# The beginning of a decoder block: first weights loaded behind the first squares, norm1_g turned between two bursts of warming matmuls, and another order of the third row tile's statistics

## Chip, cores and metric

One Trainium2 chip, one core. The metric is the device time of one execution in microseconds (us); the kernel before took 797.62 us (median of three runs, 797.24 to 797.83).

## What is computed

A decoder block on x of 512 rows and 1024 columns, in float32. The places this case is about are the first RMSNorm and the first product:

```
def rmsnorm(x, g):
    y = xf * lax.rsqrt(jnp.mean(xf * xf, axis=-1, keepdims=True) + EPS)
    return (y * g).astype(x.dtype)

h = rmsnorm(x, norm1_g[l])
z = h @ w_in[l] + b_in[l]          # 1024 x 6656
z_glu, z_rx, z_rg, z_ga, z_gb = jnp.split(z, split_idx, axis=-1)
...                                # convolution branch, RG-LRU branch, gates, mix
x = x + m @ w_mix_out[l]
h = rmsnorm(x, norm2_g[l])
x = x + (jax.nn.silu(h @ ffn_w1[l]) * (h @ ffn_w3[l])) @ ffn_w2[l]
return rmsnorm(x, norm_f_g)
```

## The kernel before

Every product is made of three matmuls in the fp32r form: each operand is split into a high part h (a cast) and a low part l (the residue), and h·h, h·l and l·h are added up. Weights come in chunks of 128 x 1024 numbers (512 KB): loaded into a `raw` buffer (four of them), cast into the high half of an `hl` buffer, and the low half is formed by a subtraction. Chunk keys `in0`, `in8`, `in1` and so on are blocks of 128 columns of w_in; `in0` is the first chunk and `in8` the second.

x lies as four row tiles of 128 rows, each in two halves of 512 columns (`x00`, `x01` are the halves of tile 0, `x10`, `x11` of tile 1; without numbers they all read `x`). A row tile's statistics are two squares with a sum on ScalarE (L550, L556; they write a scratch tile, `n1j`, that nobody reads), a small scaling on VectorE (L551), a root on ScalarE (L557) and a reciprocal on VectorE (L558); then VectorE scales both halves in place (L595). `rstd_begin` is the first square with L551, `rstd_end` the rest. `turn_half` then turns two row tiles at once on TensorE (L574, tiles `tx`), ScalarE writes the high part times norm1_g (L582, `h10h` to `h17h`) and VectorE the residue (L583, `h10l` to `h17l`). norm1_g itself comes as 8 rows of 128 and is turned into columns of the tile `par` by a transpose and a copy (`rows_turned`, L517 and L518).

The beginning is written under a manual schedule: on TensorE, ScalarE, VectorE and SyncE instructions stand in the order in which the code issues them; GpSimd's order, and everything behind this block, is set by a scheduler. Before it, 21 matmuls of ones by ones (L506, each two passes) keep TensorE busy. In the block, row tiles 0 and 1 are turned, then the first two chunks are multiplied with them (`early_mm(0, 0)` gives `z0`, `early_mm(1, 0)` gives `z8`, both L534, with the eight matmuls by the low part of the weights last), then row tiles 2 and 3 are turned and the two products are done for them. The low part of `in0` is formed on GpSimd (L119); that of `in8` on VectorE, kept back by the class `Later` and issued at L652.

All loads are issued from SyncE's queue: four for tiles 0 and 1, the rows of norm1_g, chunks `in0` and `in8` (L167), four for tiles 2 and 3, the rows of the other parameters (L483), further chunks. An instruction that waits holds up all those behind it on its engine.

Of the kernel before, what the change touches and what calls it, by code (L numbers as in the profile page):

```python
# [8 lines left out]
F32 = mybir.dt.float32  # L9
# [4 lines left out]
P = 128  # L14
T = 512
# [18 lines left out]
RAW = 4  # L34
HL = 5
AHEAD = 4
WARM = 21

FEW, MANY = 32, 112

# [13 lines left out]
ROWS = [  # L54
    ("norm1_g", 8), ("lru_lambda", 10), ("b_in", 52), ("lru_ba", 10), ("lru_bx", 10),
    ("conv_dw_b", 8), ("conv_ln_g", 8), ("conv_ln_b", 8), ("conv_b_out", 8), ("lru_conv_b", 10),
    ("norm2_g", 8), ("lru_conv_w", 40), ("conv_dw_w", 248),
]
# [28 lines left out]
def tile_block(ctx, tc, a, out):  # L87
    nc = tc.nc
    pool = lambda name, bufs, **k: ctx.enter_context(tc.tile_pool(name=name, bufs=bufs, **k))
    consts = pool("consts", 1)  # L90
    raws = pool("raws", RAW)
# [24 lines left out]
    newest = {}  # L116
# [25 lines left out]
    def wchunk(key, src, kt, cols, where="hl", lo=pool_e, after=None):  # L142
        chunks.append((key, src, kt, cols, where, lo, after))

    class Later:

        def tensor_tensor(self, **operands):
# [2 lines left out]
    def emit_chunk(copy=act.copy, lo_by=None):  # L150
        if emitted[0] == GATES_AT:
            load_gates()
        key, src, kt, cols, where, lo, after = chunks[emitted[0]]
        emitted[0] += 1
        lo = lo_by or lo
        n = kt * cols
        if where == "made":
            raw = src()
        else:
            raw = raws.tile([P, 1024], F32, tag="raw", name=f"raw_{key}")  # L160
        rv = raw[:, :n]
        if where == "made":
            pass
        elif callable(src):
            src(raw)
        else:
            newest["load"] = nc.sync.dma_start(rv.rearrange("p (k n) -> p k n", k=kt), src).ins  # L167
        if where != "long":
            hl = hls.tile([P, 2, 1024], F32R, tag="hl", name=f"hl_{key}")
            h, l, _ = split_to(hl[:, 0, :n], hl[:, 1, :n], rv, lo, copy)  # L170
            if after:
                after(rv, h)
            held[key] = (h.rearrange("p (k n) -> p k n", k=kt), l.rearrange("p (k n) -> p k n", k=kt))
        else:
            held[key] = [
                split_to(longt(f"{key}h{i}", F32R), longt(f"{key}l{i}", F32R), rv[:, i * T : (i + 1) * T], lo)
                for i in range(2)
            ]
# [323 lines left out]


    wp = bank2("warm")
    for _ in range(WARM):
        pe.matmul(wp[:, :P], ones, ones, start=True, stop=True)  # L506

    first = [i for i, (lo, _, _) in enumerate(parts) if lo < n_first]
    load_x(0)
# [3 lines left out]
    def rows_turned(c0, c1):  # L513
        pt = bank2(f"par_ps{c0}")
        for c in range(c0, c1, P):
            m = min(P, c1 - c)
            pe.transpose(pt[:, c - c0 : c - c0 + m], rowt[row_at(c)[0]][:m, :P], ident[:m, :m])  # L517
        vec.tensor_copy(par[:, c0:c1], pt[:, : c1 - c0])  # L518
        return pt
# [25 lines left out]
    def rstd_begin(half, junk):  # L545

        i = n_stats[0]
        n_stats[0] += 1
        ss, r = stats[:, i, :2], stats[:, i, 2:3]
        act.activation(junk, half, AF.Square, accum_out=ss[:, 0:1])  # L550
        vec.tensor_scalar(out=ss[:, 0:1], in0=ss[:, 0:1], scalar1=1.0 / D, scalar2=EPS, op0=ALU.mult, op1=ALU.add)  # L551
        return ss, r

    def rstd_end(begun, half, junk):
        ss, r = begun
        act.activation(junk, half, AF.Square, accum_out=ss[:, 1:2])  # L556
        act.activation(r, ss[:, 1:2], AF.Sqrt, scale=1.0 / D, bias=ss[:, 0:1])  # L557
        vec.reciprocal(r, r)  # L558
        return r

    def rstd_of(halves, junk, between=None):
        begun = rstd_begin(halves[0], junk[0])
        if between:
            between()
        return rstd_end(begun, halves[1], junk[1])
# [22 lines left out]

    h1p = [pairt(f"h1{c}") for c in range(ND)]

    def norm1_rows(t, between=None):
        junk = [shortt(f"n1j{t}{h}") for h in range(2)]
        r = rstd_of(xt[t], junk, between)
        for h in range(2):
            vec.tensor_scalar(out=xt[t][h], in0=xt[t][h], scalar1=r, scalar2=None, op0=ALU.mult)  # L595

    HALVES = [slice(0, 256), slice(256, 512)]
    EARLY = 1
# [39 lines left out]

    ET = mybir.EngineType
    with tc.manual_schedule(engines={ET.PE, ET.Activation, ET.DVE, ET.SP}):  # L640
        norm1_rows(0)
        norm1_rows(1)
        rows_turned(0, ROWS[0][1])
        emit_to(1, vec.tensor_copy)
        turn_half("tx", xt, "norm1_g", h1p, 0, [bank, bank, bank, bank2])
        later = Later()
        emit_to(2, vec.tensor_copy, later)
        load_x(2)
        load_x(3)
        for i in first[1:]:  # L650
            load_rows(i)
        norm1_rows(2, lambda: vec.tensor_tensor(**later.operands))  # L652
        norm1_rows(3)
        for i in range(len(parts)):
            if i not in first:
                load_rows(i)
        early_mm(0, 0)
        early_mm(1, 0)
        turn_half("tx", xt, "norm1_g", h1p, 1, [bank2, bank, bank])
        emit_to(3)  # L660
        early_mm(0, 1)
        lru_factors(rows_turned(ROWS[0][1], n_first)[:, 2 * P :])
        emit_to(4)
        early_mm(1, 1)
        rows_turned(n_first, n_rows)
# [625 lines left out]
```

## Time and profile before

| what | value |
|---|---|
| median of three runs | 797.62 us (797.24 to 797.83) |
| the profiled execution: its time | 797.7 us |
| the profiled execution: span from first to last instruction | 795.9 us |
| TensorE, busy share of the span | 99% |
| VectorE, ScalarE, GpSimd | 85%, 59%, 29% |
| first turning (tiles 0 and 1) begins | 8.97 us |
| second turning (tiles 2 and 3) begins | 17.28 us |

Times in rows are microseconds from the start of the span. A timeline row gives start, duration, engine, line, operation, written and read tiles, shape, count, and in brackets the idle time of the engine before it with what ended it. In grouped rows the figures behind the bar are busy time in us and the mean of one record in ns; the ones after that are idle time before the group. A record of a matmul lasts longer than the distance to the next one, since matmuls overlap. SPq is SyncE's queue of DMA issues, PEld the weight loads of TensorE.

### The profile page before, as it was taken

Reading aid. Unit: us, or ns where it says so; the run is one execution under the profiler, and the core shown is the slowest. Engines: PE = TensorE matmul, PEld = TensorE weight load, DVE = VectorE, ACT = ScalarE, POOL = GpSimd, SP = SyncE. Lnnn points to the kernel's source line nnn. Section 1 sums busy time; section 2 is a strip of 40 time slices with the busy share of each in tenths; the row PEclk is TensorE's granted clock in tenths of the full one; section 3 lists DMA queues with packets and bytes.
Section 4 is the critical chain, followed back from the end, with each engine's and each line's share of the span. In section 5 each row is a group of like instructions: output and inputs, shape, how many; then the busy total and the mean of one; then the engine's idle time right before and its main releaser. Section 6 shows DMA issues by size and latency. Waiting matters only on the chain.

```text
span 795.9 us, 12177 instructions
## 1 busy us (share of the span) xinstructions
PE 789.2 (99%) x4369; PEld 690.5 (87%) x4369; DVE 673.2 (85%) x1020; ACT 471.7 (59%) x683; POOL 228.8 (29%) x181
## 2 busy tenths in 40 slices
PE   9999999999999999999999999999999999999997
PEld 8888888888888888888888898999999999888885
DVE  6699899999989988786787889978878887889757
ACT  6646585987768855563335575545455555577443
POOL 1855766797666856030000000000000000000000
PEclk9999999999999999999999999999999999999999
DMA  6945646487555664368847545566555553676652
GB/s 213 257 130 143 187 144 208 121 247 208 173 168 173 213 182 120 128 203 263 276 160 243 172 134 158 131 171 181 155 133 133 133 133 106 210 258 207 198 173 106
DMA packets 184604, 140.29 MB, mean 176 GB/s; under 512 B 14259, under 2 KB 162143, under 8 KB 184543
## 3 DMA queue, kind: packets, MB, share of 16 engines
q1 hardware_dynamic: 183103, 134.27, 55.2%
q0 software_dynamic: 1440, 5.24, 3.5%
q8 instruction: 34, 0.56, 0.3%
q14 instruction: 27, 0.22, 0.1%
HBM read 113.79 MB, written 18.64 MB: 166 GB/s over the span
## 4 chain that ended last, share of the span: by engine, by line
PE 99%; DVE 0%; issue 0%; ACT 0%
PE z L534 36%; PE or L953 13%; PE ft L1080 7%; PE yb L534 7%; PE fa L1080 7%; PE fr L1080 6%; PE ya L534 5%; PE mxr L953 5%; PE fe L1080 4%; PE g L827 3%; PE fb L1080 2%; PE f L534 2%; PE warm L506 1%; PE f L1106 1%; PE tx L574 1%; PE th L574 0%
## 5 line engine op out<-in xcount | busy, mean ns | idle before, releaser
L702 DVE SCALAR_TENSOR_TENSOR cv<-u,par,cv 128x511 f32<-128x511 f32 (+19 forms) x240 | 162.4, 730 | 5.0 <-ACT cv L699 4.7
L119 POOL TENSOR_TENSOR hl_in<-raw_in,hl_in 128x1024 fp32r<-128x1024 f32 x51 | 123.5, 2426 | 83.1 <-ACT hl_in L123 69.6
L355 POOL DMA_DIRECT2D raw_fb<-raw_fb x10 | 8.7, 874 | 298.4 <-DVE raw_fb L357 186.1
L119 POOL TENSOR_TENSOR ows<-ows 128x256 f32<-128x256 f32 x66 | 56.7, 861 | 37.7 <-DMA ows<-in_ffn_w_dram 34.7
L123 ACT CAST hl_ft<-raw_fb 128x1024 fp32r<-128x1024 f32 x40 | 41.8, 1048 | 32.5 <-DVE raw_fb L357 17.0
L123 ACT CAST hl_in<-raw_in 128x1024 fp32r<-128x1024 f32 x50 | 52.1, 1043 | 10.4 <-PE z L534 6.6
L119 DVE TENSOR_TENSOR hl_ft<-raw_fb,hl_ft 128x1024 fp32r<-128x1024 f32 x40 | 48.5, 1220 | 7.0 <-ACT hl_ft L123 6.9
L119 DVE TENSOR_TENSOR hl_fb<-raw_fb,hl_fb 128x1024 fp32r<-128x1024 f32 x30 | 36.6, 1221 | 9.5 <-ACT hl_fb L123 9.3
L357 DVE TENSOR_TENSOR raw_fb<-raw_fb,raw_fb 128x1024 f32<-128x1024 f32 x20 | 24.5, 1225 | 20.3 <-DMA raw_fb<-in_ffn_w_dram 20.0
L534 PE MATMUL z<-h10h,hl_in 128*128 128x512 f32 (+1 forms) x108 | 41.5, 385 | 0.0
L534 PE MATMUL z<-h17h,hl_in 128*128 128x512 f32 (+1 forms) x108 | 41.1, 381 | 0.0
L534 PE MATMUL z<-h13h,hl_in 128*128 128x512 f32 (+1 forms) x108 | 41.1, 381 | 0.0
L534 PE MATMUL z<-h15h,hl_in 128*128 128x512 f32 (+1 forms) x108 | 41.1, 381 | 0.0
L534 PE MATMUL z<-h14h,hl_in 128*128 128x512 f32 (+1 forms) x108 | 41.1, 381 | 0.0
L534 PE MATMUL z<-h16h,hl_in 128*128 128x512 f32 (+1 forms) x108 | 41.1, 381 | 0.0
L534 PE MATMUL z<-h12h,hl_in 128*128 128x512 f32 (+1 forms) x108 | 41.1, 381 | 0.0
L534 PE MATMUL z<-h11h,hl_in 128*128 128x512 f32 (+1 forms) x108 | 41.1, 381 | 0.0
L123 ACT CAST hl_fb<-raw_fb 128x1024 fp32r<-128x1024 f32 x30 | 31.4, 1047 | 8.9 <-PE mxr L953 3.7
L119 DVE TENSOR_TENSOR hl_ob<-raw_ob,hl_ob 128x1024 fp32r<-128x1024 f32 (+1 forms) x23 | 27.0, 1174 | 11.0 <-ACT hl_ob L123 10.9
L123 ACT CAST hl_ob<-raw_ob 128x1024 fp32r<-128x1024 f32 (+1 forms) x23 | 23.3, 1015 | 21.6 <-PE or L953 10.8
L1080 PE MATMUL fe<-hs_0h,hl_ft 128*128 128x256 f32 x160 | 30.7, 283 | 0.0
L1080 PE MATMUL ft<-hs_1h,hl_ft 128*128 128x256 f32 x160 | 30.4, 283 | 0.0
(1016 smaller groups left out, 2610.0 us busy)
## 6 DMA issues: line engine op xcount, KB each, us to landing
raw_in<-in_w_in_dram SPq DMA_DIRECT2D x52, 512.0 KB
raw_fb<-in_ffn_w_dram SPq DMA_DIRECT2D x96, 256.0 KB
ows<-in_ffn_w_dram SPq DMA_DIRECT2D x44, 256.0 KB
os<-ows SPq DMA_DIRECT2D x22, 512.0 KB
raw_ob<-in_ffn_w_dram SPq DMA_DIRECT2D x33, 256.0 KB
raw_ot<-os SPq DMA_DIRECT2D x33, 256.0 KB
raw_lo<-in_lru_w_out_dram SPq DMA_DIRECT2D x16, 320.0 KB
raw_fb<-raw_fb POOLq DMA_DIRECT2D x10, 512.0 KB, 4.6
```

The costliest lines, as they stand in the source:

```text
L119: return eng.tensor_tensor(out=o, in0=x, in1=y, op=ALU.subtract)
L123: copy(h, full)
L355: pool_e.dma_start(out=q, in_=y, accum_op=ALU.add)
L357: vec.tensor_tensor(out=q, in0=q, in1=y, op=ALU.add)
L506: pe.matmul(wp[:, :P], ones, ones, start=True, stop=True)
L534: pe.matmul(ps, l, r, start=i == 0, stop=i == n - 1)
L574: pe.transpose(ps[:, t * P : (t + 1) * P], src, ident)
L702: vec.scalar_tensor_tensor(out=acc[c][:, s:], in0=u[c][:, : T - s], scalar=dw(c, s), in1=acc[c][:, s:], op0=ALU.mult, op1=ALU.add)
L827: pe.matmul(ps, l, r, start=k == 0, stop=k == len(mms) - 1)
L953: pe.matmul(banks[i], l_[:, ts], r_, start=start and n == 0, stop=stop and n == 2, skip_group_check=again)
L1080: pe.matmul(ps[:, HALVES[i]], lw[:, 4 * i + c, :], rx_, start=not (again or i or c or m), stop=bool(i and c == 3 and m == 2), skip_group_c ...
L1106: pe.matmul(plain_1[:, cs], l, r, start=k == 0 and m == 0, stop=k == ND - 1 and m == 2)
```

## The change

Three things change in the beginning.

1. The scratch tile of row tile 0's two squares is no longer a short tile but the first 512 columns of the raw buffers of chunks `in0` and `in8` (`weight_room`). The loads of these chunks are issued later in the code (`load_ahead`), `in0` in two pieces, and each must wait until the square that writes its buffer is done: first half and second half of `in0` behind the first square, `in8` behind the second.
2. The 21 warming matmuls become 12 and 6, and the turning of norm1_g with its copy stands between them, ahead of row tile 1's statistics in the code.
3. `Later`'s subtraction (the low part of `in8`) moves from between tile 2's first square and its reciprocal to between tile 3's first square and its reciprocal, so that tile 2's root, reciprocal and scaling stand ahead of it on VectorE.

```
-WARM = 21
+WARM = 12, 6
...
+    ahead_raw = {}
+
+    def weight_room(i):
+        key = chunks[i][0]
+        ahead_raw[key] = raws.tile([P, 1024], F32, tag="raw", name=f"raw_{key}")
+        return ahead_raw[key]
+
+    def load_ahead(i, pieces=1):
+        key, src, kt, cols = chunks[i][:4]
+        raw = ahead_raw[key]
+        for h in range(pieces):
+            ks = slice(h * kt // pieces, (h + 1) * kt // pieces)
+            to = raw[:, : kt * cols].rearrange("p (k n) -> p k n", k=kt)
+            newest["load"] = nc.sync.dma_start(to[:, ks, :], src[:, ks, :]).ins
...
-        if where == "made":
+        if key in ahead_raw:
+            raw, where = ahead_raw.pop(key), "there"
+        elif where == "made":
             raw = src()
...
-    for _ in range(WARM):
-        pe.matmul(wp[:, :P], ones, ones, start=True, stop=True)
+
+    def warm_up(n):
+        for _ in range(n):
+            pe.matmul(wp[:, :P], ones, ones, start=True, stop=True)
+
+    warm_up(WARM[0])
...
-    def norm1_rows(t, between=None):
-        junk = [shortt(f"n1j{t}{h}") for h in range(2)]
-        r = rstd_of(xt[t], junk, between)
+    def row_junk(t):
+        return [shortt(f"n1j{t}{h}") for h in range(2)]
+
+    def scale_rows(t, r):
         for h in range(2):
             vec.tensor_scalar(out=xt[t][h], in0=xt[t][h], scalar1=r, scalar2=None, op0=ALU.mult)
+
+    def norm1_rows(t, junk=None):
+        scale_rows(t, rstd_of(xt[t], junk or row_junk(t)))
...
-        norm1_rows(0)
+        junk = [weight_room(i)[:, :T] for i in range(2)]
+        norm1_rows(0, junk=junk)
+        load_ahead(0, 2)
+        load_ahead(1)
+        rows_turned(0, ROWS[0][1])
+        warm_up(WARM[1])
         norm1_rows(1)
-        rows_turned(0, ROWS[0][1])
         emit_to(1, vec.tensor_copy)
         turn_half("tx", xt, "norm1_g", h1p, 0, [bank, bank, bank, bank2])
...
-        norm1_rows(2, lambda: vec.tensor_tensor(**later.operands))
-        norm1_rows(3)
+        jk = [row_junk(t) for t in (2, 3)]
+        begun = rstd_begin(xt[2][0], jk[0][0])
+        scale_rows(2, rstd_end(begun, xt[2][1], jk[0][1]))
+        begun = rstd_begin(xt[3][0], jk[1][0])
+        vec.tensor_tensor(**later.operands)
+        scale_rows(3, rstd_end(begun, xt[3][1], jk[1][1]))
```

Line numbers of the changed kernel are higher by 17 to 33: the warming is L525 there, the turning L595 and `Later`'s subtraction L685.

VectorE from the first statistics to the first residue, before (`x_114` to `x_117` are the halves of tiles 0 and 1, `par` the turned norm1_g, `hl_in` the high part of `in0`):

```order
L551 TENSOR_SCALAR stats<-stats 128x1
L558 RECIPROCAL stats<-stats 128x1
L595 TENSOR_SCALAR x_114<-x_114,stats 128x512
L595 TENSOR_SCALAR x_115<-x_115,stats 128x512
L551 TENSOR_SCALAR stats<-stats 128x1
L558 RECIPROCAL stats<-stats 128x1
L595 TENSOR_SCALAR x_116<-x_116,stats 128x512
L595 TENSOR_SCALAR x_117<-x_117,stats 128x512
L518 COPY par<-par_ps_203 128x8
L123 COPY hl_in_208<-raw_in_206 128x1024
L583 TENSOR_SCALAR h10l<-tx_211,par,h10h 128x256
```

The same place on VectorE in the changed kernel:

```order
L572 TENSOR_SCALAR stats<-stats 128x1
L579 RECIPROCAL stats<-stats 128x1
L617 TENSOR_SCALAR x_114<-x_114,stats 128x512
L617 TENSOR_SCALAR x_115<-x_115,stats 128x512
L539 COPY par<-par_ps_188 128x8
L572 TENSOR_SCALAR stats<-stats 128x1
L579 RECIPROCAL stats<-stats 128x1
L617 TENSOR_SCALAR x_116<-x_116,stats 128x512
L617 TENSOR_SCALAR x_117<-x_117,stats 128x512
L123 COPY hl_in_206<-raw_in_176 128x1024
L604 TENSOR_SCALAR h10l<-tx_209,par,h10h 128x256
```

The copy of norm1_g moved from between tile 1's scaling and the cast of `in0` to between tile 0's scaling and tile 1's statistics.

VectorE behind the last residue of tiles 0 and 1, before (`hl_in_253` is chunk `in8`: its cast first, its low part at L652; `x_118` to `x_121` are the halves of tiles 2 and 3):

```order
L583 TENSOR_SCALAR h17l<-tx_246,par,h17h 128x256
L123 COPY hl_in_253<-raw_in_251 128x1024
L551 TENSOR_SCALAR stats<-stats 128x1
L652 TENSOR_TENSOR hl_in_253<-raw_in_251,hl_in_253 128x1024
L558 RECIPROCAL stats<-stats 128x1
L595 TENSOR_SCALAR x_118<-x_118,stats 128x512
L595 TENSOR_SCALAR x_119<-x_119,stats 128x512
L551 TENSOR_SCALAR stats<-stats 128x1
L558 RECIPROCAL stats<-stats 128x1
L595 TENSOR_SCALAR x_120<-x_120,stats 128x512
L595 TENSOR_SCALAR x_121<-x_121,stats 128x512
```

The same place in the changed kernel (the chunk is `hl_in_249` there):

```order
L604 TENSOR_SCALAR h17l<-tx_244,par,h17h 128x256
L123 COPY hl_in_249<-raw_in_177 128x1024
L572 TENSOR_SCALAR stats<-stats 128x1
L579 RECIPROCAL stats<-stats 128x1
L617 TENSOR_SCALAR x_118<-x_118,stats 128x512
L617 TENSOR_SCALAR x_119<-x_119,stats 128x512
L572 TENSOR_SCALAR stats<-stats 128x1
L685 TENSOR_TENSOR hl_in_249<-raw_in_177,hl_in_249 128x1024
L579 RECIPROCAL stats<-stats 128x1
L617 TENSOR_SCALAR x_120<-x_120,stats 128x512
L617 TENSOR_SCALAR x_121<-x_121,stats 128x512
```

The low part of `in8` moved behind the scaling of tile 2, by four instructions. On TensorE the last eight matmuls of `z8` read it and wait for it.

SyncE from the rows of norm1_g on, in the changed kernel (before, two chunk loads without a wait stood in the place of the three):

```order
L500 DMA rows_109<-in_norm_g_dram 8x128
L158 DMA raw_in_176<-in_w_in_dram 128x4x128 [waits Activation_49]
L158 DMA raw_in_176<-in_w_in_dram 128x4x128
L158 DMA raw_in_177<-in_w_in_dram 128x8x128 [waits Activation_49]
L507 DMA x_118<-in_x_dram 128x512 [waits DMAHW0_49]
L507 DMA x_119<-in_x_dram 128x512 [waits DMAHW1_49]
```

The wait is for ScalarE (Activation), and the loads of row tiles 2 and 3 stand behind it.

More of the change, by code (lines that the diff above doesn't have):

```diff
@@ L161, in emit_chunk @@
         rv = raw[:, :n]
-        if where == "made":
+        if where in ("made", "there"):
             pass
```

## The prediction

> **What bounds the kernel now.** I began with the page's engine shares, went on to TensorE's waits, then cut the span in two where the change stops, and last read the beginning instruction by instruction.
>
> From the page, the engine shares:
>
> ```profile
> span 795.9 us, 12177 instructions
> ...
> PE 789.2 (99%) x4369; PEld 690.5 (87%) x4369; DVE 673.2 (85%) x1020; ACT 471.7 (59%) x683; POOL 228.8 (29%) x181
> ```
>
> All waits of TensorE in the span, and TensorE's busy time on both sides of 17.28 us (columns: stretch, length, PE busy with its records, granted clock, DMA share, GB/s):
>
> ```profile
> PE warm L506 <- DVE ones L499: 1.1, 1, 1.1
> ```
>
> ```profile
> 0.00:17.28 17.28, 16.19 (x107) 1.00 0.63 197
> 17.28:795.90 778.62, 773.01 (x4264) 1.00 0.59 176
> ```
>
> TensorE is the bound: its one named wait is 1.1 us at the very start. The second row begins with the second turning (L574 for row tiles 2 and 3). Behind it come 778.62 us of a stream that the change leaves in its order on TensorE. So the change is worth what it moves the 17.28 us mark by, and the question is what sets that mark. The timeline there:
>
> ```profile
> 1.09 7.80 PE L506 MATMUL warm<-ones 128*128 128x128 f32 x42 [1.09 <-DVE ones L499]
> ...
> 7.83 0.88 DVE L595 TENSOR_SCALAR x<-x,stats 128x512 f32<-128x512 f32 x2
> ...
> 8.82 0.22 PE L517 MATMUL par_ps<-ident,rows 8*128 8x8 f32 x1
> ...
> 8.97 1.97 PE L574 MATMUL tx<-ident,x 128*128 128x128 f32 x16
> 9.08 0.17 DVE L518 COPY par<-par_ps 128x8 f32<-128x8 f32 x1 [0.37 <-PE par_ps L517]
> 9.16 0.68 DVE L123 CAST hl_in<-raw_in 128x1024 fp32r<-128x1024 f32 x1
> 9.45 0.47 ACT L582 ACTIVATE h10h<-tx,par 128x256 fp32r<-128x256 f32 x1 [1.85 <-PE tx L574]
> ...
> 9.93 2.40 POOL L119 TENSOR_TENSOR hl_in<-raw_in,hl_in 128x1024 fp32r<-128x1024 f32 x1 [8.62 <-DVE hl_in L123]
> 9.96 0.48 DVE L583 SCALAR_TENSOR_TENSOR h10l<-tx,par,h10h 128x256 fp32r<-128x256 f32 x1
> ...
> 12.71 0.47 DVE L583 SCALAR_TENSOR_TENSOR h17l<-tx,par,h17h 128x256 fp32r<-128x256 f32 x1
> ...
> 13.24 0.39 PE L534 MATMUL z<-h17l,hl_in 128*128 128x256 f32 x1
> ...
> 16.32 0.28 PE L534 MATMUL z<-h10h,hl_in 128*128 128x256 f32 x1
> ...
> 17.28 2.30 PE L574 MATMUL tx<-ident,x 128*128 128x128 f32 x16
> ```
>
> Row tile 1 is scaled by 8.71 (7.83 + 0.88), its first half by about 8.3, yet the turning starts at 8.97: the 21 warming matmuls (42 passes) and the turned norm1_g stand before it. From there VectorE paces. Eight residues (h10l to h17l) run back to back, the last starting 2.75 us after the first (0.39 each) and ending at 13.18, and TensorE takes it at 13.24. From 13.24 to 17.28 TensorE runs 33 products of 0.12 us without a pause: eight with the first chunk's low part, 16 with the second chunk (z8), and from 16.32 eight with z8's low part.
>
> **The change, part by part.** *Warming matmuls.* Their passes in two stretches, then what ScalarE does with row tiles 0 and 1 (records overlap, so I divide the busy time less one record by the records less one):
>
> ```profile
> L506 PE MATMUL warm<-ones 128*128 128x128 f32 x25 | 5.5, 421 | 0.0
> ```
>
> ```profile
> L506 PE MATMUL warm<-ones 128*128 128x128 f32 x12 | 1.5, 275 | 0.0
> ```
>
> ```profile
> 3.95 0.19 ACT L550 ACTIVATION_READ_ACCUMULATOR n1j<-x 128x1 f32 x1
> ...
> 4.94 0.19 ACT L556 ACTIVATION_READ_ACCUMULATOR n1j<-x 128x1 f32 x1
> ...
> 6.54 0.63 ACT L556 ACTIVATE n1j<-x 128x512 f32<-128x512 f32 x1
> ...
> 7.30 0.30 ACT L557 ACTIVATE stats<-stats 128x1 f32<-128x1 f32 x1
> ```
>
> From 2 to 7 us a pass takes (5.5 - 0.42) / 24 = 0.21 us, from 7.5 to 8.6 us (1.5 - 0.28) / 11 = 0.11. The granted clock reads 1.00 in both stretches, so I read the speed from the pace. The three matmuls taken out are six passes at the fast pace, 0.67 us. Twelve matmuls (24 passes at 0.21) end at 1.09 + 5.1 = 6.2. Then norm1_g is turned, which needs its own load. That load is queued behind row tile 1, whose second half was there by 6.54 (its square starts right behind the square before it). I put the load at 6.4 to 6.9; the trace bounds it only by 8.82, where it is used today without a wait, and that end costs 1.5 us. Then 12 passes, the first few slow: TensorE is free at 8.1 to 8.4. The first half of tile 1 is ready at about 8.3, so the turning starts at **8.3 instead of 8.97**. The copy of norm1_g (0.17) now stands ahead of tile 1's statistics on VectorE; at about 6.8 to 7.1 it lies in VectorE's wait for the root at 7.30. Without that cover it costs its 0.17.
>
> *The loads that wait.* SyncE's issues and waits:
>
> ```profile
> 0.74 1.82 SPq L490 DMA_DIRECT2D x<-in_x_dram  x4
> 2.60 0.38 SPq L483 DMA_DIRECT2D rows<-in_norm_g_dram  x1
> 3.03 1.03 SPq L167 DMA_DIRECT2D raw_in<-in_w_in_dram  x2
> 4.10 4.04 SPq L490 DMA_DIRECT2D x<-in_x_dram  x4
> ...
> 10.50 0.28 SPq L483 DMA_DIRECT2D rows<-in_lru_bx_dram  x1
> 11.19 0.27 SPq L483 DMA_DIRECT2D rows<-in_conv_dw_b_dram  x1
> 11.90 0.27 SPq L483 DMA_DIRECT2D rows<-in_conv_ln_g_dram  x1
> ```
>
> ```profile
> SPq L483 <- DMA raw_in<-in_w_in_dram: 1.2, 1, 1.2
> ```
>
> Chunk 0 now starts when the first square is read out (3.95 + 0.19 = 4.14 instead of 3.03), in two issues of about 0.5 us; chunk 8 starts at 5.13 or so instead of 3.5. Behind them on SyncE stand the loads of row tiles 2 and 3 (4.10 becomes about 5.6) and the parameter rows. Does the later start make chunk 0 land later? The 1 MB of tiles 0 and 1 goes first in the same queue and is not all there before about 6.5, so chunk 0 would sit behind it at either start. Today chunk 8 lands at 10.50 (the one wait of SyncE on raw_in); 512 KB less at about 0.31 MB/us (197 GB/s over the whole stretch, near 310 while the queue is full) is 1.7 us, so chunk 0 lands near 8.8. Its latest is 9.16, where the cast takes it without a wait; if the whole delay of 1.1 us came through, 10.3. I take 8.8, the end that the queue's order supports. Tiles 2 and 3 land from 11.19 on (SyncE waits for them one by one), and ScalarE will want the first at about 11.7: 0.5 us to spare.
>
> The cast of chunk 0 (0.68) no longer stands behind the copy of norm1_g: it runs 8.82 to 9.50 and the first residue starts at **9.50 instead of 9.96**. The high half that it needs is done by then (turning at 8.3, plus 0.99 from the rows at 8.97, 9.45 and 9.96). GpSimd's low part then ends at 9.5 + 2.4 = 11.9, a microsecond early. Gain at this point: 0.46 us, and the last residue ends at 12.72.
>
> *The third tile's statistics.* VectorE after the last residue, today:
>
> ```profile
> 13.10 0.68 DVE L123 CAST hl_in<-raw_in 128x1024 fp32r<-128x1024 f32 x1
> 13.70 0.14 DVE L551 TENSOR_SCALAR stats<-stats 128x1 f32<-128x1 f32 x1
> 13.82 1.23 DVE L652 TENSOR_TENSOR hl_in<-raw_in,hl_in 128x1024 fp32r<-128x1024 f32 x1
> 14.96 0.16 DVE L558 RECIPROCAL stats<-stats 128x1 f32<-128x1 f32 x1
> 15.15 0.88 DVE L595 TENSOR_SCALAR x<-x,stats 128x512 f32<-128x512 f32 x2
> 15.95 0.14 DVE L551 TENSOR_SCALAR stats<-stats 128x1 f32<-128x1 f32 x1
> 16.52 0.17 DVE L558 RECIPROCAL stats<-stats 128x1 f32<-128x1 f32 x1 [0.42 <-ACT stats L557]
> 16.72 0.88 DVE L595 TENSOR_SCALAR x<-x,stats 128x512 f32<-128x512 f32 x2
> ```
>
> Today the low part of chunk 8 (1.23 us, L652) hides ScalarE's root for tile 2, and the root for tile 3 leaves VectorE idle for 0.42. The change swaps this: the idle time comes at tile 2, and the low part hides the root of tile 3. VectorE's total stays; what moves is the end of the low part. From a cast at 13.10 - 0.46 = 12.64: statistics at 13.24, reciprocal 0.57 later (as 15.95 to 16.52) at 13.81, scaling at 14.01, tile 3's statistics at 14.81, the low part from 14.93 to 16.16, scaling of tile 3 from 16.26 to 17.14. TensorE would reach z8's low part at 16.32 - 0.46 = 15.86 and gets it at 16.16 + 0.06 = 16.22 (the 0.06 as from 13.18 to 13.24). **A new wait of 0.36 us takes most of the gain.** Eight products of 0.12 later the second turning starts at 17.18 instead of 17.28, with tile 3 ready.
>
> *The sum:* -0.46 + 0.36 = -0.10 us. The profiled execution took 797.7 us around its span of 795.9, 0.08 above the median of the three runs. 797.7 - 0.1 = **797.6**, no change that shows. What a measurement of this kernel can tell from no change is about 0.2%, 1.6 us, that is 796.0 to 799.2.
>
> **The rivals.**
>
> 1. *Slower: the clock.* The fast pace came 6.0 us after the first pass (1.09 to about 7.1). The new break in the warming at 6.2, 0.2 to 0.7 us of waiting and a turning of 8 rows, may start that count again. Then the fast pace comes near 6.6 + 6.0 = 12.6. The 12 passes end at 6.65 + 12 x 0.21 = 9.2, 16 transposes at twice 0.11 at 12.7, the last residue at about 13.9 instead of 12.72: +1.2, 798.8. It decides from the point where the break counts as idle. For it: the break lies just ahead of the switch. Against: it is short beside 6 us. [...]
> 2. *Slower: the weights come late.* If the delay of 1.1 us passes through, chunk 0 lands at 10.3, the first residue starts at 11.0, and the time is 797.7 + 1.04 + 0.36 = 799.1; half of it gives 798.3. For it: every packet of the weights now waits for a square. Against: the queue is full until then.
> 3. *Faster: the new wait does not come.* If tile 2's squares and root are earlier relative to VectorE, or VectorE starts its cast sooner because tiles 0 and 1, now alone in the queue, land sooner (tile 1's first square waits for its load today, up to 0.36 us), the gain of 0.46 survives: 797.2, at best 796.9.
>
> **How the numbers follow.** Forecast (797.2 to 798.0) 72%; rival 1 11%; rival 2 7%; rival 3 10%. The range leaves out the upper part of rivals 1 and 2 and a rest: 796.9 to 798.7. More than 1.6 us is beyond the price of every case: faster 2%, since even a turning at 8.3 saves at most 0.7; slower 5%, where the clock stays slow into the products or rivals 1 and 2 add up; same 93%.
>
> **What would show it.** The turning of tiles 0 and 1 at 8.3; the cast of chunk 0 straight behind the scaling of tile 1 with no wait for its load above 0.2; the first residue at 9.5; TensorE (its weight loads) waiting for hl_in of VectorE by 0.3 to 0.5 ahead of z8's last eight; the second turning within 0.3 of 17.28. Passes of 0.21 behind 7.5 us would mean rival 1, a wait of VectorE for raw_in rival 2. The forecast is wrong if the stream behind the second turning changes its length: VectorE's and SyncE's orders shift slightly there, and I count that at nothing since TensorE's only named wait is at the start.

## The result and the profile after

| | median | range | executions |
|---|---|---|---|
| before | 797.77 us | 797.03 to 799.26 | 20 |
| after | 799.04 us | 798.37 to 799.83 | 20 |

The ratio is 1.0015 (95% interval 1.0009 to 1.0022). The changed kernel is 1.27 us slower: less than the 0.2% named in the prediction, but 1.4 us above the forecast of 797.6 and 0.34 us above the end of the range.

The profiled execution took 799.77 us around a span of 798.0, so it is one of the longer ones. The page of the changed kernel, engine shares:

```profile
span 798.0 us, 12167 instructions
...
PE 789.1 (99%) x4363; PEld 689.9 (86%) x4363; DVE 673.2 (84%) x1020; ACT 471.9 (59%) x683; POOL 229.2 (29%) x181
```

TensorE is busy for 789.1 us as against 789.2 before; the 2.1 us more of span are idle time. All waits of TensorE's matmuls in the changed kernel (engine, tile, line, what it waits for; us in total, times, longest):

```profile
PE warm L525 <- DVE ones L516: 1.1, 1, 1.1
PE fr L1113 <- ACT ft L1213: 1.0, 1, 1.0
PE z L555 <- DVE hl_in L685: 0.5, 1, 0.5
PE z L555 <- DVE h10l L604: 0.3, 1, 0.3
```

There was one wait before; there are four now. The span cut at the second turning, which stood at 17.28 before (columns as in the prediction's table of stretches, with all engines):

```profile
0.00:17.90 17.90, 16.03 (x101) 14.75 (x102) 10.38 (x30) 11.22 (x31) 3.10 (x7) 1.00 0.58 187
17.90:798.00 780.10, 773.06 (x4264) 675.16 (x4262) 662.85 (x990) 460.73 (x652) 226.15 (x174) 1.00 0.60 176
```

The mark comes 0.62 us later, and the stretch behind it is 780.10 us instead of 778.62 with the same busy time on TensorE (773.06, 773.01). So the prediction missed in two places: the mark (+0.62, forecast -0.10) and the stream behind it (+1.48, forecast nothing). The beginning of the changed kernel in time, with the rows that answer to those of before:

```profile
1.09 5.49 PE L525 MATMUL warm<-ones 128*128 128x128 f32 x24 [1.09 <-DVE ones L516]
...
4.64 1.50 SPq L158 DMA_DIRECT2D raw_in<-in_w_in_dram  x3
...
6.53 0.25 PE L538 MATMUL par_ps<-ident,rows 8*128 8x8 f32 x1
...
6.71 1.60 PE L525 MATMUL warm<-ones 128*128 128x128 f32 x12
...
6.82 0.17 DVE L539 COPY par<-par_ps 128x8 f32<-128x8 f32 x1
...
7.67 0.88 DVE L617 TENSOR_SCALAR x<-x,stats 128x512 f32<-128x512 f32 x2
...
8.15 1.91 PE L595 MATMUL tx<-ident,x 128*128 128x128 f32 x16
...
9.20 0.69 DVE L123 CAST hl_in<-raw_in 128x1024 fp32r<-128x1024 f32 x1 [0.65 <-DMA raw_in<-in_w_in_dram]
...
9.81 0.48 DVE L604 SCALAR_TENSOR_TENSOR h10l<-tx,par,h10h 128x256 fp32r<-128x256 f32 x1
...
12.03 0.28 SPq L500 DMA_DIRECT2D rows<-in_lru_bx_dram  x1
...
12.75 0.63 ACT L571 ACTIVATE n1j<-x 128x512 f32<-128x512 f32 x1 [1.15 <-DMA x<-in_x_dram]
12.95 0.69 DVE L123 CAST hl_in<-raw_in 128x1024 fp32r<-128x1024 f32 x1
...
13.44 0.63 ACT L577 ACTIVATE n1j<-x 128x512 f32<-128x512 f32 x1
13.54 0.15 DVE L572 TENSOR_SCALAR stats<-stats 128x1 f32<-128x1 f32 x1
...
14.52 0.16 DVE L579 RECIPROCAL stats<-stats 128x1 f32<-128x1 f32 x1 [0.83 <-ACT stats L578]
...
15.58 1.21 DVE L685 TENSOR_TENSOR hl_in<-raw_in,hl_in 128x1024 fp32r<-128x1024 f32 x1
...
16.85 0.39 PE L555 MATMUL z<-h10h,hl_in 128*128 128x256 f32 x1 [0.50 <-DVE hl_in L685]
...
17.90 2.29 PE L595 MATMUL tx<-ident,x 128*128 128x128 f32 x16
```

The turning stands at 8.15, as forecast, and the copy of norm1_g is hidden ahead of tile 1's statistics. But VectorE then waits 0.65 us for chunk 0, so the first residue starts at 9.81. SyncE waits 1.6 us for the first square, the loads of tiles 2 and 3 behind it are issued from 6.19 on instead of 4.10, SyncE is done waiting for chunk 8 at 12.03 instead of 10.50, and ScalarE waits 1.15 us for row tile 2 (12.75). Its root is therefore late, VectorE idles 0.83 us in front of tile 2's reciprocal, the low part of chunk 8 ends at 16.79, and TensorE waits 0.50 us for it.

### The profile page after: what moved, and what is told of

Its sections match the earlier page's. It is cut to its first block, busy times and chain, and to the rows that moved or that the text cites. A ratio compares the mean times of both kernels' runs of the same rounds, so it can differ in the third digit from the quotient of the medians.

```text
span 798.0 us, 12167 instructions
## 1 busy us (share of the span) xinstructions
PE 789.1 (99%) x4363; PEld 689.9 (86%) x4363; DVE 673.2 (84%) x1020; ACT 471.9 (59%) x683; POOL 229.2 (29%) x181
## 4 chain that ended last, share of the span: by engine, by line
PE 91%; DMA 5%; DVE 3%; ACT 1%; issue 1%; SPq 0%; DVEq 0%; POOLq 0%; ACTq 0%
PE z L555 35%; PE or L986 13%; PE yb L555 7%; PE fa L1113 6%; PE ft L1113 6%; PE ya L555 5%; PE mxr L986 5%; PE g L860 3%; PE fr L1113 3%; PE fe L1113 3%; PE fb L1113 2%; DMA raw_fb<-raw_fb 2%; PE f L555 1%; DMA raw_fb<-in_ffn_w_dram 1%; DMA x<-in_x_dram 1%; DVE raw_fb L374 1%
## 5 line engine op out<-in xcount | busy, mean ns | idle before, releaser
L735 DVE SCALAR_TENSOR_TENSOR cv<-u,par,cv 128x511 f32<-128x511 f32 (+17 forms) x240 | 162.5, 731 | 5.0 <-ACT cv L732 4.8
```

The costliest lines, as they stand in the source:

```text
L735: vec.scalar_tensor_tensor(out=acc[c][:, s:], in0=u[c][:, : T - s], scalar=dw(c, s), in1=acc[c][:, s:], op0=ALU.mult, op1=ALU.add)
```

## The experiments

The change has three parts, called here *loads* (they wait for the squares), *warming* (12 and 6 around the turned norm1_g) and *low part* (behind tile 2's scaling). The theory after the result: the beginning is longer because the low part comes late and the later loads give back what the shorter warming gains; something at the end of the program adds to it. Rivals: the beginning is longer by one part alone; the clock; a changed order of the stream behind the beginning; or nothing but scatter. Sixteen kernels were measured, each beside the kernel before on the same chip: e1 to e4 on one chip, e5 to e8 on a second, e9 to e16 on a third.

| kernel | loads | warming | low part | median us (range, n) | ratio to before, 95% |
|---|---|---|---|---|---|
| e1_later_back | yes | yes | | 799.10 (797.52 to 802.83, 12) | 1.0013 [1.0001, 1.0025] |
| e12, the same | yes | yes | | 798.22 (797.22 to 798.92, 11) | 1.0003 [0.9994, 1.0011] |
| e2_loads_only | yes | | | 798.52 (797.64 to 799.72, 11) | 1.0006 [0.9998, 1.0015] |
| e3_warming_only | | yes | | 798.52 (797.46 to 802.06, 12) | 1.0009 [1.0000, 1.0019] |
| e4_later_only | yes | | yes | 798.68 (797.85 to 799.74, 11) | 1.0006 [0.9998, 1.0015] |
| e11_low_part_only | | | yes | 798.66 (797.73 to 799.25, 11) | 1.0008 [0.9999, 1.0017] |
| e9_before_again | | | | 797.88 (797.48 to 798.76, 11) | 1.0002 [0.9993, 1.0011] |
| e10_changed_again | yes | yes | yes | 798.84 (798.02 to 799.50, 11) | 1.0011 [1.0003, 1.0020] |
| e13_one_piece | one piece | yes | yes | 799.15 (797.85 to 800.80, 11) | 1.0019 [1.0010, 1.0027] |
| e15, one piece | one piece | yes | | 798.08 (797.50 to 799.60, 11) | 1.0007 [0.9998, 1.0016] |
| e14_one_load_more | two pieces, no wait | | | 797.89 (797.52 to 799.26, 11) | 1.0005 [0.9997, 1.0014] |

Kernels e5 to e8 and e16 hold the beginning alone, and their medians are of some 32 us. They leave out the scatter behind the beginning, which in the full kernels makes intervals of some 0.7 us to either side; their own executions still differ by 0.4 to 1.5 us.

**e1 and e12: the low part put back.** The edit to the changed kernel (e12 is the same program a second time):

```
         begun = rstd_begin(xt[2][0], jk[0][0])
+        vec.tensor_tensor(**later.operands)
         scale_rows(2, rstd_end(begun, xt[2][1], jk[0][1]))
         begun = rstd_begin(xt[3][0], jk[1][0])
-        vec.tensor_tensor(**later.operands)
```

> The changed kernel with the low part of the second chunk put back ahead of row tile 2's root (loads and warming stay changed). Theory: of the 0.62 us by which the second turning came later in the changed kernel (17.90 against 17.28), the move of the low part is the cause of nearly all, by TensorE's wait of 0.5 ahead of z8's last eight and by VectorE's idle 0.83 ahead of tile 2's reciprocal. Then the second turning comes back to 17.1 to 17.3 and the time falls by 0.6 to 0.8 from 799.0 to about 798.3. Rival: the late loads of row tile 2 (its first square waited 1.15 us) set the second turning whatever the order on VectorE; then it stays at 17.7 or later and the time at 798.8 to 799.1.

> Loads and warming changed, low part in its old place, once more (the first series scattered from 797.5 to 802.8). The order behind the beginning is that of the kernel before. Theory: 0.1 to 0.5 above the kernel before, as the cut kernel's 0.4. Rival (order): below e10_changed_again by 0.8 or more.

Measured: 799.10 and 798.22. e1 lies where the rival put it, e12 (0.40 above before) where the theory did; the intervals overlap and cannot say whether the low part alone makes the difference. The traces can: from the first residue to the second turning it takes 7.32 us in e1 (10.42 to 17.74) and 7.33 in e12 (9.57 to 16.90), as before (9.96 to 17.28), and 8.10 after (9.81 to 17.90). That stretch hangs on the low part: in all 18 profiles it is 7.32 to 7.43 in the eleven kernels that have it in its old place and 7.68 to 8.10 in the seven where it is moved. The first residue itself moves by 0.85 us between two executions of one program. In e1's execution there was also a wait at 181 us, taken up below.

**e2: loads alone; e3: warming alone.** e2 is e1 with the warming of before:

```
-WARM = 12, 6
+WARM = 21, 0
...
-        rows_turned(0, ROWS[0][1])
-        warm_up(WARM[1])
         norm1_rows(1)
+        rows_turned(0, ROWS[0][1])
```

e3 is e1 with the loads of before:

```
-        junk = [weight_room(i)[:, :T] for i in range(2)]
-        norm1_rows(0, junk=junk)
-        load_ahead(0, 2)
-        load_ahead(1)
+        norm1_rows(0)
```

> The kernel before with only the loads changed (they wait for the first squares; 21 warming matmuls in one piece, low part of the second chunk in its old place). Theory: the first residue is set by the warming as before (9.96), tile 2's later landing (near 12.7) is hidden behind the cast and the low part, the second turning comes at 17.3 to 17.5, and the time is 797.8 to 798.1. Rival: what the beginning does not explain in the changed kernel (about 0.7 us behind the second turning) comes from the whole queue of loads being 1.4 us later; then the time is 798.4 to 798.8 with the second turning hardly moved.

> The kernel before with only the warming changed (12 and 6 with the turning of norm1_g between; loads start without a wait; low part in its old place). Theory: the first turning starts at 8.2 to 8.4, chunk 0 is there by then or soon after, the first residue starts at 9.4 to 9.6 and everything follows: second turning at 16.8 to 16.9, time 797.3 to 797.5. [...]

Both 798.52, neither told apart from before with certainty (1.0006 and 1.0009; the lower end of e3's interval is at 1.0000). Neither gained anything: e2's median lies in the range of its rival (798.4 to 798.8), e3's 1.0 us above the end of its theory (797.3 to 797.5). e3's profiled execution took 802.06 us, 3.5 above its median, so its trace is not the usual one. e2 has its first residue at 9.94, where it was; e3 at 11.08, since TensorE waited 1.7 us for norm1_g and then ran at half its clock for 3.4 us (last section).

**e4: loads and low part; e11: low part alone.** e4 is the changed kernel with the first of these two diffs (it has the waiting loads beside the moved low part), e11 with both of them.

> The changed kernel with the warming of before (21 matmuls in one piece, norm1_g turned behind them); loads and the low part stay changed. Theory: first residue at 9.96 to 10.1, second turning 0.3 to 0.4 later than in the changed kernel's profile less what its late chunk cost, 18.0 to 18.2; time 799.1 to 799.4. Rival: warming does not matter since the landing of chunk 0 sets the first residue in both; second turning at 17.9, time 799.0 as in the changed kernel.

> The kernel before with only the low part of the second chunk moved; the scheduler's order behind the beginning (convolution on VectorE, four loads on SyncE) then is that of the changed kernel. Theory (the move costs its wait of 0.36 and no more): second turning at 17.6 to 17.7, 0.3 to 0.5 above the kernel before. Rival (the order behind the beginning costs 0.7): 0.9 to 1.2 above it.

798.68 and 798.66, 0.6 and 0.8 us above before on the same chips. From the first residue to the second turning: 7.82 us in e4, 7.70 in e11. The low part costs 0.38 (7.70 - 7.32) with nothing else changed. In time neither kernel met its forecast: e4 is faster than the theory and the rival had it, and e11's 0.84 lies between the two, with an interval (-0.1 to 1.4) that holds both. e11's profile speaks against its rival: behind the beginning SyncE's order is that of the changed kernel, and from the second turning to the end of the span it takes 778.58 us, before 778.62. The changed order cost nothing in that execution.

**e5 to e8 and e16: the beginning alone.** To the kernels before (e5), after (e6), e1 (e7), e3 (e8) and e11 (e16) this was added behind `rows_turned(n_first, n_rows)`; everything behind the two first products is left out:

```
+    for i, (m, _, ps) in enumerate(early):
+        o = longt(f"end{m}")
+        act.copy(o, ps)
+        nc.sync.dma_start(o_nat[:, i, :T], o)
+    return
```

> The beginning of the kernel before alone: it ends behind the first two products of all rows and stores these two tiles, everything else is left out. It gives the base for the next three. Theory (the change costs time in the beginning, and the second turning of the kernel before varies with the instant at which the clock is released): the times spread over about 0.7 us, some 30 to 45 us in all. Rival (the beginning costs only 0.6, the rest of the 1.27 us comes behind it): no statement on the base.

> The beginning of the changed kernel alone, cut in the same way. Theory: 0.9 to 1.3 us above e5_start_before, so that the whole change of 1.27 us lies in the beginning. Rival (part of it lies behind the beginning, in loads or in the scheduler's order): 0.3 to 0.7 us above it.

> The beginning alone with the changed loads and warming, the low part of the second chunk back in its old place. Theory (the low part's place costs most): 0.6 to 0.9 below e6_start_after, within 0.3 of e5_start_before. Rival (the late loads cost most): within 0.3 of e6_start_after.

> The beginning alone with only the warming changed. Theory: 0.2 to 0.5 below e5_start_before, since TensorE is free and the copy of norm1_g out of the way earlier. Rival (the break in the warming holds back the clock, or the turned norm1_g waits for its load): 0 to 1 above it.

> The cut beginning of the kernel before with only the low part of the second chunk moved. Theory (its wait of 0.36 is the whole of its cost and the main cost of the change in the beginning): 0.3 to 0.5 above e5_start_before's 32.2, that is 32.5 to 32.7. Rival (the late tiles cost as much): 32.2 to 32.4.

| beginning alone | median us | range, n |
|---|---|---|
| e5 before | 32.21 | 31.86 to 32.69, 6 |
| e8 warming | 32.27 | 31.82 to 32.96, 6 |
| e16 low part | 32.59 | 32.54 to 32.92, 5 |
| e7 loads and warming | 32.63 | 31.73 to 33.18, 6 |
| e6 all three | 32.79 | 32.70 to 33.66, 6 |

The beginning of the changed kernel costs 0.58 us more by the medians, and the ranges of e5 and e6 just do not touch. But e5's executions fall into two groups, near 31.9 and near 32.6, so the size depends on which are compared: by the quickest execution of each it is 0.84. That the beginning is slower is shown, and its size is 0.6 to 0.8 us. The same holds for the low part alone, 0.38 by the medians and 0.68 by the quickest, and e16 ran on another chip than e5; its size is better read from the rows below. The warming gains nothing (+0.06 and -0.04) where 0.2 to 0.5 was expected. Loads and warming (e7) scatter over 1.45 us and are not resolved; the median is nearer to e6, as its rival had it. e5 from its first residue to the second turning:

```profile
9.95 0.48 DVE L604 SCALAR_TENSOR_TENSOR h10l<-tx,par,h10h 128x256 fp32r<-128x256 f32 x1
...
17.29 2.29 PE L595 MATMUL tx<-ident,x 128*128 128x128 f32 x16
```

And e16, where only the low part is moved:

```profile
9.70 0.48 DVE L604 SCALAR_TENSOR_TENSOR h10l<-tx,par,h10h 128x256 fp32r<-128x256 f32 x1
...
14.01 0.17 DVE L579 RECIPROCAL stats<-stats 128x1 f32<-128x1 f32 x1 [0.42 <-ACT stats L578]
...
15.07 1.22 DVE L681 TENSOR_TENSOR hl_in<-raw_in,hl_in 128x1024 fp32r<-128x1024 f32 x1
...
16.34 0.19 PEld L555 LDWEIGHTS z<-h10h,hl_in 128*128 128x128 f32 x1 [0.31 <-DVE hl_in L681]
...
17.40 2.29 PE L595 MATMUL tx<-ident,x 128*128 128x128 f32 x16
```

7.34 us in e5, 7.70 in e16: 0.36 more, the term of the prediction to a hundredth, and at the place that it named: TensorE's weight load waits 0.31 us for the low part. VectorE's idle time in front of tile 2's reciprocal is 0.42 in e16 and 0.83 in the changed kernel; the difference of 0.41 is the rest of its 8.10 (7.32 + 0.37 + 0.41).

**e9 and e10: before and after once more,** both written with the helpers of the changed kernel: e9 is e11 with e1's edit, e10 has no edit.

> The kernel before once more, written through the changed helpers; its instructions are the same on every engine. It shows the scatter: what two series of one program differ by, and whether the stalls of TensorE near 181 us (gate product waiting for ext6h) and 541 us (product waiting for ScalarE's copy behind a late weight load) that the changed kernels' profiles show come without any change too. Theory (those stalls are scatter of the loads): ratio within 0.1% of 1 and, in its profile, one of the two stalls or none, depending on the execution. Rival (the stalls come from the change): none of them, stream behind the second turning 772.6 us.

> The changed kernel once more, beside the others. Theory (beginning costs about 0.6 us by the cut kernels, the rest of the 1.27 is scatter): 0.5 to 0.9 us above the kernel before on this chip. Rival (0.7 us more lie behind the beginning, in the order that the scheduler made there): 1.1 to 1.5 above it.

797.88 and 798.84 beside 797.82 for before: the slowdown comes back at 1.02 us, between what the theory and the rival of e10 expected, and scatter as the whole explanation falls. e10's profiled execution took 798.99, close to its median, so it is nearer to the usual one than the first profile of the changed kernel:

```profile
9.70 0.48 DVE L604 SCALAR_TENSOR_TENSOR h10l<-tx,par,h10h 128x256 fp32r<-128x256 f32 x1
...
14.34 0.16 DVE L579 RECIPROCAL stats<-stats 128x1 f32<-128x1 f32 x1 [0.76 <-ACT stats L578]
...
17.73 2.29 PE L595 MATMUL tx<-ident,x 128*128 128x128 f32 x16
```

8.03 us, with tile 2 late again (0.76 of idle time). e9's, which is the program before, shows that this program varies too (the last row is cut by the view's window):

```profile
1.09 7.10 PE L525 MATMUL warm<-ones 128*128 128x128 f32 x42 [1.09 <-DVE ones L516]
...
8.27 2.23 PE L595 MATMUL tx<-ident,x 128*128 128x128 f32 x16
8.65 1.62 PEld L595 LDWEIGHTS tx<-ident,x 128*128 128x128 f32 x15 [0.24 <-DVE x L617]
...
8.98 0.68 DVE L123 CAST hl_in<-raw_in 128x1024 fp32r<-128x1024 f32 x1
...
9.67 0.48 DVE L604 SCALAR_TENSOR_TENSOR h10l<-tx,par,h10h 128x256 fp32r<-128x256 f32 x1
...
17.00 1.25 PE L595 MATMUL tx<-ident,x 128*128 128x128 f32 x10
```

The 42 passes take 7.10 us here and 7.80 in the execution of the prediction, so the turning starts at 8.27 with the old warming, and waits for tile 1 as well. The first residue is at 9.67, earlier than in the changed kernel's two profiles (9.81, 9.70).

**e13, e14, e15: the end of the program.** The last matmul starts at 789.91 in before and 791.56 after; to the end of the span it is 6.00 and 6.44 us. What lies there is the last store and SyncE's waits. SyncE's waits for the stores in that stretch, for before and then after (us in total, times, longest):

```profile
SPq L1287 <- DMA out_dram<-of: 1.3, 2, 0.7
```

```profile
SPq L1320 <- DMA out_dram<-of: 1.8, 1, 1.8
```

SyncE ends the program by waiting for eight counters of landed transfers, in the same order in the four traces below, and a wait that is satisfied already takes 0.06 us. The trace's instructions there, with two kernels that follow below:

```
          last store issued   its counter   wait for it ends   other waits behind it       end of span
before    792.75              8th           795.03             none                        795.9
after     794.41              1st           796.70             seven, 796.77 to 797.13     798.0
e13       794.59              8th           796.88             none                        797.8
e14       793.69              1st           795.99             seven, 796.05 to 796.41     797.3
```

From issue to landing it is 2.3 us in all four; from there to the end of the span 0.9 us in before and e13, 1.3 in after and e14. Loads and stores take the counters in turn: in the traces the last two stores of before signal on the 7th and the 8th, the last three of after on the 7th, the 8th and the 1st. With one load more (`in0` comes in two pieces) the last store sits on the counter that is waited for first, and the other seven waits, 0.43 us from 796.70 to 797.13, come after its landing instead of before it. Three kernels test this. e13 is an edit to the changed kernel, e15 the same edit to e1:

```
-        load_ahead(0, 2)
+        load_ahead(0)
```

e14 is the kernel before with the load of `in0` in two pieces and no wait:

```
-            newest["load"] = nc.sync.dma_start(rv.rearrange("p (k n) -> p k n", k=kt), src).ins
+            to, pieces = rv.rearrange("p (k n) -> p k n", k=kt), 2 if key == "in0" else 1
+            for i in range(pieces):
+                ks = slice(i * kt // pieces, (i + 1) * kt // pieces)
+                newest["load"] = nc.sync.dma_start(to[:, ks, :], src[:, ks, :]).ins
```

> The changed kernel with in0 loaded in one piece: one load fewer on SyncE, all else as changed. Theory of the lanes (SyncE counts its transfers' ends on eight semaphores in turn and ends the program by waiting for all eight in a fixed order; one load more at the beginning moves the last store to the first of the eight, so that seven waits of 0.06 us follow its landing): from the last matmul's start to the end of the span 6.00 instead of 6.44, the time 0.4 below e10_changed_again, 0.5 to 0.8 above the kernel before. Rival (the 0.43 at the end comes from where the last store happens to land): 6.44 stays.

> The kernel before with in0 loaded in two pieces, without any wait; nothing else differs on any engine. Theory of the lanes: 6.43 from the last matmul's start to the end, the beginning as before (second turning 16.9 to 17.3), the time 0.4 above the kernel before. Rival: 6.00 and no difference.

> Loads that wait and the split warming, but in0 in one piece and the low part in its old place: the change without its two costs. Theory: 6.00 at the end, second turning at 16.8 to 17.3, the time within 0.3 of the kernel before. Rival (the late loads themselves cost): 0.4 or more above it.

SyncE's last waits in e13, then in e14:

```profile
SPq L1320 <- DMA out_dram<-of: 1.3, 2, 0.7
```

```profile
SPq L1319 <- DMA out_dram<-of: 1.8, 1, 1.8
```

The end takes 6.00 us in e13 and e15, 6.44 in e14. In the profiles of all eleven full kernels and of before and after it is 6.43 or 6.44 where there is one load more (after, e1, e2, e4, e10, e12, e14) and 6.00 or 6.01 where there is not (before, e3, e9, e11, e13, e15). So the 0.43 us are shown, and they have nothing to do with the weights' wait. In time e13 gained nothing: 799.15. Its chunk 0, in one piece behind the square, was cast only at 10.37 and its first residue came at 10.98; e15's at 10.56. Both are single executions. e15, which was to be the change without its two costs, is 0.43 us above before, where its rival (the late loads themselves cost) put it, and its second turning stands at 17.88 instead of 16.8 to 17.3. Its interval, -0.2 to 1.3, does not settle what the late loads cost in time. e14's median is 0.24 above before, with an interval from -0.2 to 1.1: it agrees with 0.43 and does not show it.

**What is left.** In the changed kernel's first profile the account is nearly full: of the 2.10 us by which its span is longer, 0.62 lie at the second turning, 0.44 at the end and 0.99 in TensorE's wait at 541 us. The medians give less: 0.58 to 0.84 from the beginning and 0.43 from the end make 1.0 to 1.3 of the 1.27 us, so that the wait at 541 us may or may not have a share in the usual execution. There a load of ffn weights lands late, VectorE waits 3.56 us for it (row of the changed kernel; 3.26 before, where TensorE is not held up), ScalarE's cast comes late, and TensorE stands for 1.0 us:

```profile
539.43 1.23 DVE L374 TENSOR_TENSOR raw_fb<-raw_fb,raw_fb 128x1024 f32<-128x1024 f32 x1 [3.56 <-DMA raw_fb<-in_ffn_w_dram]
```

e10 has 0.3 us of it, e12 0.4. e14, whose stream behind the beginning is that of before in order, has nearly as much as the changed kernel:

```profile
PE fr L1112 <- ACT ft L1212: 0.8, 1, 0.8
```

So a changed order of the stream is not its cause. It is absent in before, e9, e11 and e4 and present in the nine other full kernels, always at the same place, and its size varies from 0.2 to 1.0 us. Whether the altered first 20 us bring it out at 541 us, and how often the kernel before has it, stays open: there is one profiled execution of each kernel. The same holds for a wait at 181 us, which stands in the profiles of e1 to e4 (0.8 to 2.3 us) and in no other; these four also ran on a chip of their own.

## Why the prediction was wrong

Two steps of the sum failed: the gain of 0.46 us at the first residue, of which the runs show 0.05, and the stream behind the second turning, counted at nothing, which was 1.48 us longer in the profile and whose end took 0.43 us more in every profile of a kernel with one load more.

*The turning at 8.3:* right, 8.15. The six passes fewer and the hidden copy of norm1_g came as worked out. norm1_g was turned at 6.53, inside the forecast 6.4 to 6.9 (6.13 to 7.67 in the other kernels with this warming). But as a gain the step from 8.97 was in large part an accident of the profile before: with the old warming the turning stands at 8.27 in e9.

*The gain at the first residue, -0.46:* this failed, for two reasons. First, "the queue is full until then" was wrong. DMA rates over 5 to 7 us, before and then after (last figure, GB/s):

```profile
5.00:7.00 2.00, 2.00 (x11) 2.00 (x10) 1.20 (x4) 1.60 (x6) 0.00 (x0) 1.00 1.02 324
```

```profile
5.00:7.00 2.00, 2.00 (x11) 1.75 (x11) 1.23 (x5) 1.89 (x7) 0.00 (x0) 1.00 0.67 213
```

The two tiles ran out before the first weights came: from 5.5 to 6.0 us the rate was 85 GB/s, and 295 before. That is 2 x (324 - 213) = 222 KB less in the 2 us, 0.7 us at 0.32 MB/us. Chunk 0 was usable at 9.20 instead of 8.8, chunk 8 was waited for until 12.03 instead of 10.50. That is the condition of rival 2, met in part at chunk 0 and in full behind it. Second, 9.96 was one execution's value. e5, e9, e14, e11 and e16, which keep the warming of before and loads without a wait, have 9.95, 9.67, 9.97, 10.29 and 9.70 (with 9.96 a mean of 9.92); the kernels with waiting loads in two pieces and the new warming (after, e10, e6, e7, e1, e12) have 9.81, 9.70, 9.75, 10.00, 10.42 and 9.57 (mean 9.88). Of 0.46 us there is 0.05 left, less than the scatter of either.

*The new wait for chunk 8's low part, 0.36:* right in mechanism and size. Rows with only this part changed give 0.36 to 0.38.

*"0.5 us to spare" for tiles 2 and 3:* failed. It was measured from landings at 11.19, which the late queue moved too; tile 2 came at 12.75. That costs 0.41 us in the changed kernel's profile, 0.34 in e10's and 0.12 in e4's, though nothing in e6 and e13, whose loads wait as well.

*The stream behind, counted at nothing:* failed. The end of the program costs 0.43, by the count of loads, which I did not follow to where SyncE waits for it. The wait at 541 us adds some tenths in e10's usual execution.

*The sum:* the change gave +1.27 instead of -0.10. Of the 1.37 us between them, some 0.4 are the gain that did not come and 0.43 the end of the program; about 0.5 is left for the late tile 2 and the wait at 541 us, which the profiles show and no median separates; how it divides stays open.

*Rivals:* rival 1 did not happen in this kernel: behind the break the 12 passes took 1.60 us, the fast pace (the first excepted). The range takes in a lower part of rival 1; that is an estimate of mine, which no run shows. What the runs show of the clock behind a break is e3, where it stood at a half for 3.4 us and the execution took 802.06 us (last section). Rival 2 named the price of the late weights as 798.3 to 799.1 (half of its 1.40 us is 0.70, which makes 798.4) and was given 7%; it was nearest, but partly by luck, since the end of the program has no place in its sum. Rival 3 did not happen.

## What to carry to other kernels

When a transfer is made to wait, follow the queue and not only its first user: with the bytes that are under way and the rate, work out when the queue runs dry, and move every later landing by that gap (here the rate fell to 85 GB/s from 5.5 to 6.0 us, and chunk 8 came 1.53 us later). A gain that is read as the distance between two marks of one profiled execution is worth no more than the marks repeat from one execution to the next; where a mark hangs on when a clock is released (3.9 to 7.3 us over these profiles), take a second execution before you count it. And a change in the number of transfers can move the end of the program, here by 0.43 us, so look at the waits behind the last store as well.

## What the runs showed of the hardware

*The clock's release.* The pace of the warming passes changes from 0.21 to 0.11 us at about 7.1 in before and 5.6 in e9, the same program. By the trace's clock records the granted clock goes up at 7.09 in before and 6.65 after, and over the 18 profiles at anywhere between 3.9 and 7.3 us; what sets the instant is not shown. So the warming matmuls bind only in late executions, before's profile being one of the latest; in e9, e11, e14 and e16, which have the old warming and an early clock, the turning waits for row tile 1 instead (its weight loads for 0.24, 1.16, 0.59 and 0.47 us).

*The clock's loss.* In e3 TensorE stood from 5.92 to 7.67 for norm1_g, and later the clock was halved. A row of the break, and e3's stretches from 6.8 on (granted clock third from the end):

```profile
7.67 0.19 PE L538 MATMUL par_ps<-ident,rows 8*128 8x8 f32 x1 [1.75 <-DMA rows<-in_norm_g_dram]
```

```profile
6.80:8.40 1.60, 0.73 (x6) 0.74 (x7) 0.43 (x3) 1.37 (x5) 0.00 (x0) 1.00 1.15 336
8.40:9.80 1.40, 1.40 (x9) 1.40 (x9) 1.22 (x4) 0.12 (x1) 0.00 (x0) 0.53 1.11 309
9.80:11.80 2.00, 2.00 (x11) 2.00 (x11) 1.15 (x3) 1.23 (x3) 1.49 (x1) 0.50 1.05 379
11.80:13.20 1.40, 1.40 (x14) 1.40 (x13) 1.40 (x5) 1.40 (x5) 0.88 (x1) 0.96 0.30 98
```

For 3.4 us, from 8.49 to 11.90 by the trace's clock records, the clock stands at a half: rival 1 as a fact, though in another kernel. The loss begins 0.82 us behind the end of the break of 1.75 us. e8, with a break of 1.22 us at the same place, kept its clock: it reads 1.00 from 5.0 to 11.8, and the 12 passes behind the break took 1.60 us (2.32 in e3). In e12 and e13, which have the changed kernel's warming, TensorE waited 1.0 and 1.2 us for norm1_g, and the 12 passes took 1.60 us as well: below 1.75, but not by much.

*A wait that costs twice.* e1's profiled execution took 802.83 us, 3.7 above its median. TensorE's wait at 181 us, and the clock behind it:

```profile
PE g L860 <- DMA ext6h<-xb7h: 2.3, 1, 2.3
```

```profile
183.60:187.00 3.40, 3.30 (x8) 2.70 (x9) 3.26 (x6) 1.62 (x2) 3.09 (x5) 0.51 0.53 163
```

The 2.3 us of waiting are followed by 3.4 us at half the clock, with 0.43 us from one matmul to the next instead of 0.23, which by estimate (half of 3.4) costs another 1.7. A wait of 1.8 us at the same place in e3, from 182.1 to 183.9, left the clock alone: 0.23 us from matmul to matmul behind it. Why one wait cost the clock and the other did not is not shown. They differ in length, and by estimate in where they lie against the clock records: these stand, within one execution, whole steps of 3.41 us apart (in e1 at 6.05, 183.55 and 186.96, which is 52 steps and one more; in before at 7.09 and 795.57, which is 231). By estimate, counted on from e3's 8.49, a step ends at 182.6, early in e3's wait; e1's ends at 183.55, just ahead of the end of its wait at 183.70.
